# Merge gates and branch projections of a two-layer mixer, from feature-major to token-major

## The chip, the cores and the metric

One Trainium2 chip, one of its cores. The metric is the device time of one launch in microseconds (us). Three runs of the kernel before took 942.8, 944.91 and 942.83 us, median 942.83 us.

## The reference, cut to what matters

The program is a decoder trunk of two layers over 256 tokens of 1024 features in float32. Each layer has a token mixer with three branches (A: gated linear recurrence, B: gated delta rule, C: gated linear attention), each of which gives 256x512 values, and then a SwiGLU feed-forward part; a layer norm follows each of the two. The change sits where the mixer's branches are merged:

```
gates  = sigmoid(p_merge + gate_b)               # p_merge = x @ w_in[..., 3 x 1024 columns]
merged = sum(gates[:, :, gi] * (y @ w_branch[gi]) for gi, y in enumerate((ya, yb, yc)))
mix    = merged @ w_out                          # 256 x 1024
x      = layer_norm(alpha * x + mix)
```

So per layer there are three gate projections (1024 to 1024), three branch projections (512 to 1024), a product and a sum, and the output projection (1024 to 1024), called wo below.

## The kernel before, in words

**Precision.** A matmul operand a is kept as two rounded parts, a = hi + lo, and each product is three matmuls: hi by hi, lo by hi, hi by lo. Weights stream from memory in units of 128x1024 (512 KB): a DMA on SP's queue brings `raw` (4 buffers), ScalarE (ACT) copies it rounded to `hi`, and VectorE (DVE) subtracts to get `lo` (for some units in the middle of a layer GpSimd, POOL, does the subtraction instead). `unit()` hands the parts to the matmuls, and `fill()` splits units ahead of use: 6 ahead (`AHEAD`), and 14 (`FAR`) from the first branch unit of the third branch on. What is split ahead needs two of the 37 slots of 4 KB per partition, and `raw` of a later unit is fetched when an earlier one is split.

**Two orders of a matmul.** In `fm_acc` a 128x128 block of weights is the stationary operand and 256 tokens of the activations move past it: the result has features on the partitions (feature-major). In `tm_acc` a 128x128 block of activations (128 tokens) is stationary and 512 weight columns move past it: the result has tokens on the partitions (token-major), and there is one bank of PSUM for each half of the tokens (tk 0 and 1).

**The merge.** Before, gates and branches go by `fm_acc`. A gate unit pair ends in `g_chain`: ACT adds the bias, one value per partition, and takes the sigmoid in one instruction of 128x256, straight from PSUM into `gt`. A branch unit (two feature tiles, 24 matmuls) ends in `m_chain` for j = 0 to 3: DVE multiplies the PSUM tile with the gate, and from the second branch on adds it to the sum `macc`; after the third branch it splits `macc` into `mh` hi (ACT) and lo (DVE), since the sum already has features on the partitions, which is what wo needs for its stationary operand. Branches go in the order A, C, B. The list `MIX` gives the order of units.

**wo.** Its eight units go by `tm_acc`, column half n outer, the 256-row block q inner. Block q needs `mrg{q}`, the split of the quarter q of the sum, so that wo starts on the first quarter while the last is still on its way. A layer norm chain `ln_chain` for each tk follows the two halves n.

**What sets the order.** A planner (`Order.drive`) interleaves the main chain of matmuls with the spawned chains by estimated costs, and a scheduler sets the final order in which each engine issues. An engine works through its instructions in that order: one that waits holds up all behind it.

Of the kernel before, what the change touches and what calls it, by code (L numbers as in the profile page):

```python
# [20 lines left out]
P = 128  # L21
# [10 lines left out]
C_PAX, C_PAG, C_QKV, C_Z, C_SB, C_SA = 0, 512, 1024, 2560, 3072, 3076  # L32
C_CQ, C_CK, C_CV, C_CG, C_CR, C_MG = 3080, 3336, 3592, 4104, 4120, 4632

V_AW, V_AB, V_BR, V_BI, V_LAM, V_BW, V_BN, V_CG, V_CN, V_GB, V_AL, V_SM = (
    0, 16, 20, 24, 28, 32, 80, 81, 83, 84, 108, 112)
NV = 113

K_ID, K_U, K_RS, K_LM, K_BD, K_B16, K_D8, K_M32 = 0, 128, 256, 512, 768, 896, 912, 920
NK = 952  # L40


MIX = ("c0 c1 ax0 k0 k1 q0 z0 q1 ax1 v0 v1 ag0 ag1 gA0 gA1 gA2 gA3 bA0 bA1 bA2 bA3 "
       "gC0 bC0 gC1 bC1 gC2 bC2 gC3 bC3 gB0 gB1 bB0 bB1 gB2 bB2 gB3 bB3").split()
BRANCHES = "ACB"
MODE = 2

# [1 line left out]
def stream_order():  # L49
    fm = lambda c, j: [("fm", c + P * (2 * j + t)) for t in range(2)]  # L50
    tm = lambda c: [("tm", c, q) for q in range(4)]
    o = tm(C_CV) + tm(C_CR)
    base = {"q": C_QKV, "k": C_QKV + 512, "v": C_QKV + 1024, "ax": C_PAX, "ag": C_PAG,
            "c": C_CQ}
    for u in MIX:
        nm, i = u[:-1], int(u[-1])
        if nm == "z":
            o += tm(C_Z)
        elif nm in base:
            o += fm(base[nm], i)  # L60
        else:
            b = "ABC".index(nm[1])
            o += fm(C_MG + 1024 * b, i) if nm[0] == "g" else [("br", b, i)]
    o += [("wo", n, q) for n in range(2) for q in range(4)]
    o += [("f1t", q) for q in range(4)] + [("f3t", q) for q in range(4)]
    for f in range(4, NF):
        o += [("f1", f), ("f3", f)]
    o += [("f2", j) for j in range(NF)]
    return o
# [6 lines left out]
def pack(inp):  # L76
    a = {k: np.asarray(v) for k, v in inp.items()}
    f = np.float32
    w = np.empty((L, NU, P, 1024), f)
    for l in range(L):  # L80
        w_in = a["w_in"][l]
        for i, u in enumerate(ORDER):
            q = u[-1]
            if u[0] == "fm":
                src, sh = w_in[:, u[1]:u[1] + P], (8, P, P)
            elif u[0] == "tm":
                src, sh = w_in[256 * q:256 * q + 256, u[1]:u[1] + 512], (2, P, 512)
            elif u[0] == "br":
                src, sh = a["w_branch"][l, u[1]][:, 256 * q:256 * q + 256], (4, P, 256)
            elif u[0] == "wo":  # L90
                src = a["w_out"][l][256 * q:256 * q + 256, 512 * u[1]:512 * u[1] + 512]
                sh = (2, P, 512)
            elif u[0] in ("f1t", "f3t"):
                src = a["ffn_w" + u[0][1]][l][256 * q:256 * q + 256, 0:512]
                sh = (2, P, 512)
            elif u[0] == "f1":
                src, sh = a["ffn_w1"][l][:, P * q:P * q + P], (8, P, P)
            elif u[0] == "f3":
                src, sh = a["ffn_w3"][l][:, P * q:P * q + P], (8, P, P)
            else:  # L100
                src, sh = a["ffn_w2"][l][P * q:P * q + P], (1, P, D)
            w[l, i].reshape(P, sh[0], sh[2])[...] = src.reshape(sh).transpose(1, 0, 2)
    cols = list(range(C_CG, C_CG + 16)) + list(range(C_SB, C_SB + 8))
    wsm = np.ascontiguousarray(
        a["w_in"][:, :, cols].reshape(L, 8, P, 24).transpose(0, 2, 1, 3))
    vec = np.zeros((L, P, NV), f)

    def fm(x):
        return x.reshape(-1, P).T

    for l in range(L):
        v = vec[l]
        for t in range(4):
            v[:, V_AW + 4 * t:V_AW + 4 * t + 4] = fm(a["a_conv_w"][l, t])
            v[:, V_BW + 12 * t:V_BW + 12 * t + 12] = fm(a["b_conv_w"][l, t])
        v[:, V_AB:V_AB + 4] = fm(a["a_conv_b"][l])
        v[:, V_BR:V_BR + 4] = fm(a["a_b_r"][l])
        v[:, V_BI:V_BI + 4] = fm(a["a_b_i"][l])
        v[:, V_LAM:V_LAM + 4] = fm(a["a_lambda"][l])
        v[:, V_BN:V_BN + 1] = fm(a["b_norm_w"][l])  # L120
        v[:, V_CG:V_CG + 2] = fm(a["c_b_g2"][l])
        v[:, V_CN:V_CN + 1] = fm(a["c_norm_w"][l])
        v[:, V_GB:V_GB + 24] = fm(a["gate_b"][l])
        v[:, V_AL:V_AL + 4] = a["b_a_log"][l][None, :]
        v[20:24, V_SM] = a["b_dt_bias"][l]
    i = np.arange(P)
    kc = np.zeros((P, NK), f)
    kc[:, K_ID:K_ID + P] = i[:, None] == i[None, :]
    kc[:, K_U:K_U + P] = i[:, None] <= i[None, :]
    kc[:, K_RS:K_RS + 256] = (np.arange(256) % 64 != 0)[None, :]  # L130
    blk = lambda s: (i[:, None] // (2 * s) == i[None, :] // (2 * s)) & (
        i[:, None] // s != i[None, :] // s)
    for n, s in enumerate((8, 16)):
        kc[:, K_LM + P * n:K_LM + P * n + P] = blk(s) & (i[:, None] < i[None, :])
    j = np.arange(32)
    kc[:, K_BD:K_BD + P] = i[:, None] // 8 == i[None, :] // 8
    kc[:, K_B16:K_B16 + 16] = i[:, None] // 8 == np.arange(16)[None, :]
    kc[:, K_D8:K_D8 + 8] = i[:, None] % 8 == np.arange(8)[None, :]
    kc[:, K_M32:K_M32 + 32] = (i[:, None] % 32 // 8 == j[None, :] // 8) & (
        i[:, None] > j[None, :] + i[:, None] // 32 * 32)  # L140
    x = a["x"][0]
    return {
        "xtm": np.ascontiguousarray(x.reshape(2, P, D).transpose(1, 0, 2)),
        "xfm": np.ascontiguousarray(x.T.reshape(8, P, S).transpose(1, 0, 2)),
        "w": w, "wsm": wsm, "vec": vec,
        "aw": np.ascontiguousarray(np.stack([a["a_w_r"], a["a_w_i"]], 1)),
        "wg2": np.ascontiguousarray(a["c_w_g2"]),
        "lnv": np.ascontiguousarray(np.stack(
            [a["ln1_g"], a["ln1_b"], a["ln2_g"], a["ln2_b"]], 1)),
        "kc": kc,  # L150
    }
# [98 lines left out]
def _build(ctx, nc, tc, ins, out):  # L250
# [249 lines left out]
    def layer(l, xs, xtok):  # L500
# [504 lines left out]
            done("ya")  # L1005


        def g_chain(ps, b, j):
            ps = p2(ps)
            if j % 2 == 0:  # L1010
                B["gt", b, 0], B["gt", b, 1] = pair2("gt")
            gt = B["gt", b, j % 2]
            for t in range(2):
                act_fn(gt[:, t], ps[:, t], AF.Sigmoid, bias=vc(V_GB + 8 * b + 2 * j + t))
            B["gg", b, j] = gt
            done(f"gt{b}{j}")
            return
            yield

        def m_chain(ps, n, b, j, mh, ml):  # L1020
            yield k_(f"gt{b}{j}")
            ps = p2(ps)
            gt = B["gg", b, j]
            if n == 0:
                if j % 2 == 0:
                    B["macc", j], B["macc", j + 1] = pair2("macc")
                tt(B["macc", j], ps, gt, MULT)
            else:
                tt(gt, ps, gt, MULT)
                tt(B["macc", j], B["macc", j], gt, ADD)  # L1030
            if n == 2:
                split(mh[j], ml[j], B["macc", j])
                done(f"mrg{j}")

        def ln_chain(tk, halves, lv, xs_out, is_out, name):
            g, b = lv
# [159 lines left out]
        def main():  # L1196
# [17 lines left out]
            for u in MIX:  # L1214
# [7 lines left out]
                elif nm == "ag":  # L1222
                    yield from fm_pair(lambda ps: a_gate(ps, i), 1)
                elif nm == "z":
                    yield from tm_group(xs, [lambda ps, tk: silu_tm(ps, "sz", tk)], None)
                elif nm[0] == "g":
                    b = "ABC".index(nm[1])
                    yield from fm_pair(lambda ps: g_chain(ps, b, i), 1)
                else:
                    n, b = BRANCHES.index(nm[1]), "ABC".index(nm[1])  # L1230
                    if n == 2:
                        ahead[0] = FAR
                    y = ("ya", "yb", "yc")[b]
                    yield k_(y)
                    y = B[y]
                    w = unit(4)
                    ps = bank("br")
                    for t in range(2):
                        fm_acc(p2(ps)[:, t], w, y, slice(P * t, P * t + P))
                    O.spawn(m_chain(ps, n, b, i, mh, ml), 1)  # L1240
                    yield
                seen.append(u)
                if u in ("c1", "k1") and "c1" in seen and "k1" in seen:
                    O.spawn(b_inv(), 2)
# [12 lines left out]
            pw = [[bank("wo") for _ in range(2)] for _ in range(2)]  # L1257
            for tk in range(2):
                O.spawn(ln_chain(tk, pw[tk], lv, x1, False, "x1"), 0)
            seq = [(n, q) for n in range(2) for q in range(4)]  # L1260

            def wo(i, w, tk):
                n, q = seq[i]
# [3 lines left out]

            tail = 6
            for i in range(8 - tail):
                yield k_(f"mrg{i}")  # L1270
                w = unit(2)
                for tk in range(2):
                    wo(i, w, tk)
            u = []
            for tk in range(2):
                for i in range(8 - tail, 8):
                    if tk == 0:
                        if i < 4:
                            yield k_(f"mrg{i}")
                        u.append(unit(2, 1))  # L1280
                    else:
                        held[0] -= 1
# [182 lines left out]
```

## Time and profile before

| what | us |
|---|---|
| median of three runs | 942.83 |
| profiled execution, whole | 939.84 |
| its span in the trace | 938.0 |
| TensorE (PE) busy | 922.5 (98% of the span) |
| DVE busy | 644.5 (69%) |
| ACT busy | 523.6 (56%) |
| POOL busy | 162.4 (17%) |

The times worked with below come from the profiled execution. A matmul's own duration in the rows includes its way through the array and overlaps the next one, so the pace of a stream is read from the chain of waits, which lists stretches of matmuls with their count and length. The merge runs from about 160 to 262 us in the first layer and from about 618 to 722 us in the second.

### The profile page before, as it was taken

The page shows a single profiled execution, that of the slowest core. Times are in us where ns is not written, and L with a number is a line of the kernel's source. Part 1 is how long each engine was busy: PE and PEld are TensorE (multiplying, and loading weights), DVE is VectorE, ACT ScalarE, POOL GpSimd, SP SyncE. Part 2 cuts the span into 40 slices and gives each one's busy share as a digit, 9 for nine tenths or more (in the row PEclk, how much of TensorE's full clock was granted, in tenths as well). Part 3 has the DMA queues.
Part 4 walks back from the last instruction along what each step waited for, and adds up shares of the span by engine and source line. Part 5 has one row for each costly group of instructions (what it writes and reads, how often), then busy time and mean ns, then how long its engine had stood idle before and what let it go on. Part 6 is the DMA issues. An engine that isn't in the chain of part 4 may idle for free.

```text
span 938.0 us, 15814 instructions
## 1 busy us (share of the span) xinstructions
PE 922.5 (98%) x6306; PEld 838.3 (89%) x6306; DVE 644.5 (69%) x965; ACT 523.6 (56%) x824; POOL 162.4 (17%) x81
## 2 busy tenths in 40 slices
PE   7999999999999999999999999999999999999996
PEld 5998899999988888888889998999999888888885
DVE  5577975695875776676457699586768648667715
ACT  5877669644733665555145774973547147566600
POOL 0454512530000000000033351253300000000001
PEclk9999999999999999999999999999999999999998
DMA  8854324546770865568325352255568338655801
GB/s 273 266 182 148 101 69 130 173 149 234 249 290 3 299 215 180 182 240 275 111 72 191 121 158 96 72 155 195 181 217 280 132 117 271 219 180 180 286 7 45
DMA packets 47994, 162.84 MB, mean 174 GB/s; under 512 B 7537, under 2 KB 8497, under 8 KB 47793
## 3 DMA queue, kind: packets, MB, share of 16 engines
q1 hardware_dynamic: 47776, 161.71, 51.6%
q8 instruction: 49, 0.80, 0.3%
q14 instruction: 25, 0.20, 0.1%
q10 hardware_dynamic: 144, 0.13, 0.0%
HBM read 160.77 MB, written 1.05 MB: 173 GB/s over the span
## 4 chain that ended last, share of the span: by engine, by line
PE 92%; DVE 5%; DMA 1%; issue 1%; ACT 1%; POOL 0%; SPq 0%; POOLq 0%
PE fm L347 26%; PE f L347 22%; PE w L347 13%; PE tm L347 11%; PE br L347 7%; PE wo L347 5%; PE pt L347 1%; PE pp L347 1%; DVE sub L304 1%; DMA raw<-in_w_dram 1%; DVE lo L304 1%; PE pr L347 1%; PE px L355 1%; PE pln L355 1%; DVE xa L315 1%
## 5 line engine op out<-in xcount | busy, mean ns | idle before, releaser
L304 DVE TENSOR_TENSOR lo<-raw,hi 128x1024 fp32r<-128x1024 f32 (+1 forms) x241 | 310.0, 1305 | 108.9 <-ACT hi L292 101.7
L292 ACT ACTIVATE hi<-raw 128x1024 fp32r<-128x1024 f32 (+1 forms) x293 | 300.8, 1053 | 86.0 <-DMA raw<-in_w_dram 75.8
L347 PE MATMUL fm<-x,hi 128*128 128x256 f32 x1536 | 283.4, 286 | 0.0
L347 PEld LDWEIGHTS fm<-x,hi 128*128 128x128 f32 x1536 | 239.8, 192 | 2.1 <-issue 1.8
L347 PE MATMUL fm<-x,lo 128*128 128x256 f32 x768 | 217.7, 283 | 0.0
L347 PE MATMUL f<-x,hi 128*128 128x512 f32 x576 | 202.0, 396 | 0.0
L432 POOL TENSOR_TENSOR lo<-raw,hi 128x1024 fp32r<-128x1024 f32 x52 | 134.4, 2587 | 230.9 <-ACT hi L292 225.6
L347 PE MATMUL f<-x,lo 128*128 128x256 f32 x576 | 160.7, 279 | 0.0
L347 PEld LDWEIGHTS fm<-x,lo 128*128 128x128 f32 x768 | 147.4, 192 | 0.0
L347 PEld LDWEIGHTS f<-x,hi 128*128 128x128 f32 x576 | 108.1, 188 | 26.1
L347 PE MATMUL w<-hi,hh 128*128 128x512 f32 (+1 forms) x396 | 111.2, 367 | 0.0
L347 PEld LDWEIGHTS f<-x,lo 128*128 128x128 f32 x576 | 108.5, 188 | 0.1
L347 PE MATMUL tm<-hi,x 128*128 128x512 f32 x320 | 101.3, 400 | 3.6 <-ACT hi L292 3.6
L339 POOL TENSOR_TENSOR rs<-rs,mhalf 128x1 f32<-128x1 f32 x8 | 7.5, 936 | 524.2 <-DVE rs L309 524.2
L347 PEld LDWEIGHTS w<-hi,hh 128*128 128x128 f32 x396 | 71.4, 189 | 12.2
L347 PEld LDWEIGHTS tm<-hi,x 128*128 128x128 f32 x320 | 59.5, 191 | 17.0 <-ACT hi L292 5.2
L347 PE MATMUL w<-lo,hh 128*128 128x512 f32 (+1 forms) x198 | 72.4, 366 | 0.0
L347 PE MATMUL tm<-lo,x 128*128 128x512 f32 x160 | 62.3, 392 | 0.0
L347 PEld LDWEIGHTS w<-lo,hh 128*128 128x128 f32 x198 | 37.3, 188 | 6.2
L292 ACT ACTIVATE x<-pln 128x256 fp32r<-128x256 f32 x24 | 7.9, 383 | 60.7 <-PE pln L355 60.7
L347 PE MATMUL wo<-hi,mh 128*128 128x512 f32 x128 | 39.8, 392 | 0.0
L292 ACT ACTIVATE gt<-fm,vecs 128x256 f32<-128x256 f32 x48 | 20.3, 468 | 33.7 <-PE fm L347 33.6
(277 smaller groups left out, 1151.7 us busy)
## 6 DMA issues: line engine op xcount, KB each, us to landing
raw<-in_w_dram SPq DMA_DIRECT2D x291, 512.0 KB, 4.4
lnv<-in_lnv_dram SPq DMA_DIRECT2D x8, 512.0 KB, 7.4
xr<-in_xtm_dram SPq DMA_DIRECT2D x1, 1024.0 KB, 7.5
xin<-in_xfm_dram SPq DMA_DIRECT2D x3, 256.0 KB, 7.6
raw<-in_w_dram SPq DMA_DIRECT2D x2, 256.0 KB, 3.5
ar<-in_aw_dram SPq DMA_DIRECT2D x8, 64.0 KB, 4.2
out_dram<-xr SPq DMA_DIRECT2D x2, 256.0 KB, 2.1
kc<-in_kc_dram SPq DMA_DIRECT2D x1, 476.0 KB, 9.3
```

The costliest lines, as they stand in the source:

```text
L292: ins_ = A.activation(o, i, f, **k)
L304: V.tensor_tensor(out=o, in0=a, in1=b, op=op)
L315: V.scalar_tensor_tensor(out=o, in0=a, scalar=s, in1=b, op0=op0, op1=op1)
L339: G.tensor_tensor(out=o, in0=i, in1=e, op=ALU.pow)
L347: T.matmul(o, w, x, start=start, stop=stop)
L355: T.transpose(o, i, idn)
L432: G.tensor_tensor(out=lo, in0=t, in1=hi.bitcast(F32), op=SUB)
```

## The change

Gates and branch projections become token-major. The gate's bias now lies along the free dimension, so it is loaded per branch as a tile `gbias` that repeats the row on all partitions (one more DMA of 128x1024 values per branch and layer, on SP's queue), DVE adds it to the PSUM tile, and ACT takes the sigmoid from SBUF to SBUF, 128x512 at a time. A branch has two column halves j of two units each, and each half fills two banks of PSUM, one per tk. The product with the gate and the sum are done per tk on 128x512. After the third branch, each 128x512 piece of the sum (j, tk) is turned by four transposes on TensorE into a bank `pmt`, and from there split by two pairs of instructions of 128x256 into `mh`. wo goes with q outer and n inner, and waits for `mrg{j}{tk}`.

```
-MIX = ("... gA0 gA1 gA2 gA3 bA0 bA1 bA2 bA3 gC0 bC0 gC1 bC1 gC2 bC2 gC3 bC3 gB0 gB1 bB0 bB1 gB2 bB2 gB3 bB3")
+MIX = ("... gA0 gA1 bA0 bA1 gC0 bC0 gC1 bC1 gB0 gB1 bB0 bB1")
...
-        def g_chain(ps, b, j):
-            ps = p2(ps)
-            if j % 2 == 0:
-                B["gt", b, 0], B["gt", b, 1] = pair2("gt")
-            gt = B["gt", b, j % 2]
-            for t in range(2):
-                act_fn(gt[:, t], ps[:, t], AF.Sigmoid, bias=vc(V_GB + 8 * b + 2 * j + t))
...
+        def g_tm(ps, b, j, tk, bias):
+            if tk == 0:
+                B["gt", b, j] = pair("gt")
+            gt = B["gt", b, j][tk]
+            tt(gt, ps, bias[:, 512 * j:512 * j + 512], ADD)
+            yield
+            act_fn(gt, gt, AF.Sigmoid)
+            done(f"gt{b}{j}{tk}")
...
-            if n == 2:
-                split(mh[j], ml[j], B["macc", j])
-                done(f"mrg{j}")
+            tt(gt, ps, gt, MULT)
+            acc = B["macc", tk][j]
+            tt(acc, acc, gt, ADD)
+            if n == 1:
+                return
+            yield
+            pt = h4(bank("pmt"))
+            for q in range(4):
+                tp(pt[:, q], acc[:, q * P:(q + 1) * P], ident)
+            for q in range(2):
+                split(*(x[2 * j + q][:, :, tk * P:(tk + 1) * P] for x in (mh, ml)),
+                      pt[:, 2 * q:2 * q + 2])
+            done(f"mrg{j}{tk}")
...
-                    yield from fm_pair(lambda ps: g_chain(ps, b, i), 1)
+                    if i == 0:
+                        bias = slot("gbias")
+                        nc.sync.dma_start(out=bias, in_=ins["gb"][
+                            l:l + 1, 1024 * b:1024 * b + 1024].to_broadcast([P, 1024]))
+                    yield from tm_group(xs, [
+                        lambda ps, tk: g_tm(ps, b, i, tk, bias)], None)
...
-                    w = unit(4)
-                    ps = bank("br")
-                    for t in range(2):
-                        fm_acc(p2(ps)[:, t], w, y, slice(P * t, P * t + P))
-                    O.spawn(m_chain(ps, n, b, i, mh, ml), 1)
-                    yield
+                    ps = [bank("br") for _ in range(2)]
+                    for q in range(2):
+                        w = unit(2)
+                        for tk in range(2):
+                            tm_acc(ps[tk], y, tk, w, 2 * q, q == 0, q == 1)
+                        if q:
+                            for tk in range(2):
+                                O.spawn(m_tm(ps[tk], n, b, i, tk, mh, ml), 1)
+                        yield
...
-            seq = [(n, q) for n in range(2) for q in range(4)]
+            seq = [(n, q) for q in range(4) for n in range(2)]
...
-                yield k_(f"mrg{i}")
+                yield k_("mrg00"), k_("mrg01")
...
+                    if seq[i][1] == 2:
+                        yield k_(f"mrg1{tk}")
```

Counted over the whole program: 864 gate and branch matmuls of 256 columns per layer become 432 of 512 columns, with the same units of weights; each layer gets 16 transposes of 128x128, 12 bias additions of 128x512 on DVE and 3 DMAs more; 24 sigmoids of 128x256 become 12 of 128x512; 4 pairs of splits of 128x512 become 8 of 128x256.

PE at the end of the merge in the first layer, before. `br_3121` is the last branch tile, `mh_375` to `mh_378` are the four quarters of the split sum, `wo_...` the banks of wo, `hi_` and `lo_` the weights.

```order
L347 MATMUL br_3121<-ybh_2386,hi_2851 128x256 x2
L347 MATMUL br_3121<-ybh_2386,lo_2852 128x256
L347 MATMUL wo_3161<-hi_2857,mh_375 128x512 x2
L347 MATMUL wo_3161<-lo_2858,mh_375 128x512
L347 MATMUL wo_3161<-hi_2857,mh_375 128x512 x2
```

The same place on PE in the changed kernel. `br_2674` and `br_2675` are the two banks (tk 0 and 1) of the last branch column half, `macc_2131` and `macc_2133` the sums of tk 0 and tk 1, `kc_73` holds the identity.

```order
L349 MATMUL br_2675<-hi_2549,ybh_2223 128x512 x2
L349 MATMUL br_2675<-lo_2550,ybh_2223 128x512
L357 MATMUL pmt_2737<-kc_73,macc_2131 128x128 x4
L357 MATMUL pmt_2746<-kc_73,macc_2133 128x128 x4
L357 MATMUL pmt_2755<-kc_73,macc_2131 128x128 x4
L357 MATMUL pmt_2764<-kc_73,macc_2133 128x128 x4
L349 MATMUL wo_2726<-hi_2567,mh_375 128x512
L349 MATMUL wo_2728<-hi_2567,mh_375 128x512
```

Between the last branch matmul and the first of wo there are now 16 transposes, which read `macc`, and wo's first matmul reads an `mh` that comes from them; before, it read one that had been split while other branch units ran.

DVE from the product of the last branch unit on, before. `gt_3051` is the last gate tile, `lo_` are weight splits for units ahead.

```order
L304 TENSOR_TENSOR mh_377<-macc_2300,mh_377 128x512
L304 TENSOR_TENSOR gt_3051<-br_3121,gt_3051 128x512
L304 TENSOR_TENSOR macc_2300<-macc_2300,gt_3051 128x512
L304 TENSOR_TENSOR lo_3168<-raw_3024,hi_3167 128x1024
L304 TENSOR_TENSOR lo_3186<-raw_3059,hi_3185 128x1024
L304 TENSOR_TENSOR lo_3204<-raw_3089,hi_3203 128x1024
L304 TENSOR_TENSOR mh_378<-macc_2300,mh_378 128x512
```

DVE at the same place in the changed kernel, from the second instruction after the first product of branch B (`gt_2526<-br_2585`, column half 0, tk 0) on.

```order
L306 TENSOR_TENSOR gt_2653<-tm_2506,gbias_2426 128x512
L306 TENSOR_TENSOR gt_2653<-tm_2507,gbias_2426 128x512
L306 TENSOR_TENSOR lo_2657<-raw_2621,hi_2656 128x1024
L306 TENSOR_TENSOR macc_2131<-macc_2131,gt_2526 128x512
L306 TENSOR_TENSOR lo_2677<-raw_2627,hi_2676 128x1024
L306 TENSOR_TENSOR gt_2526<-br_2586,gt_2526 128x512
L306 TENSOR_TENSOR lo_2699<-raw_2633,hi_2698 128x1024
L306 TENSOR_TENSOR macc_2133<-macc_2133,gt_2526 128x512
L306 TENSOR_TENSOR gt_2653<-br_2674,gt_2653 128x512
L306 TENSOR_TENSOR gt_2653<-br_2675,gt_2653 128x512
L306 TENSOR_TENSOR macc_2131<-macc_2131,gt_2653 128x512
L306 TENSOR_TENSOR macc_2133<-macc_2133,gt_2653 128x512
```

Ahead of these rows stand the product `gt_2526<-br_2585` and two more `lo`; behind them come the halves of `mh` from `pmt`. So between the first product of branch B's column half 0 and the last sum there are now five weight splits and the two bias additions of the next gate tile, and the second layer has the same order.

## Rows read from the trace of the kernel before

**Rows 1.** The page, busy time, share of the span and instructions of each engine.

```profile
PE 922.5 (98%) x6306; PEld 838.3 (89%) x6306; DVE 644.5 (69%) x965; ACT 523.6 (56%) x824; POOL 162.4 (17%) x81
```

**Rows 2.** The page, shares of the span in the chain that ended last.

```profile
PE 92%; DVE 5%; DMA 1%; issue 1%; ACT 1%; POOL 0%; SPq 0%; POOLq 0%
```

**Rows 3.** Windows of the merges: length, busy us, granted clock, DMA share, GB/s.

```profile
147.80:262.10 114.30, 114.30 (x1009) 113.86 (x1010) 83.33 (x97) 68.91 (x95) 27.41 (x13) 1.00 0.59 195
585.80:722.40 136.60, 136.60 (x1220) 135.58 (x1220) 95.56 (x112) 87.08 (x126) 33.65 (x13) 1.00 0.55 181
```

**Rows 4.** The chain of waits: start us, length us, engine, tile, line, count.

```profile
71.29 10.91 PE tm L347 x48
...
116.13 1.24 DVE Y L304
...
124.67 0.87 PE pyf L355 x8
...
180.59 11.51 PE br L347 x96
...
227.53 11.52 PE fm L347 x96
239.04 5.76 PE br L347 x48
...
262.08 19.97 PE wo L347 x88
282.06 0.58 PE pln L355 x4
```

**Rows 5.** DVE's timeline, end of the first merge: start us, length us, instruction, count.

```profile
245.50 2.35 DVE L304 TENSOR_TENSOR lo<-raw,hi 128x1024 fp32r<-128x1024 f32 x2
247.77 0.68 DVE L304 TENSOR_TENSOR gt<-br,gt 128x512 f32<-128x512 f32 x1
248.37 1.21 DVE L304 TENSOR_TENSOR lo<-raw,hi 128x1024 fp32r<-128x1024 f32 x1
...
264.34 0.68 DVE L304 TENSOR_TENSOR mh<-macc,mh 128x512 fp32r<-128x512 f32 x1
264.94 0.68 DVE L304 TENSOR_TENSOR gt<-br,gt 128x512 f32<-128x512 f32 x1
265.66 0.69 DVE L304 TENSOR_TENSOR macc<-macc,gt 128x512 f32<-128x512 f32 x1
...
270.67 0.68 DVE L304 TENSOR_TENSOR mh<-macc,mh 128x512 fp32r<-128x512 f32 x1
```

**Rows 6.** ACT and DVE timelines, a split of 128x256 from transposed PSUM.

```profile
300.02 0.38 ACT L292 ACTIVATE hh<-pht 128x256 fp32r<-128x256 f32 x1 [2.55 <-PE pht L355]
300.44 0.42 DVE L304 TENSOR_TENSOR hh<-pht,hh 128x256 fp32r<-128x256 f32 x1 [2.18 <-ACT hh L292]
```

**Rows 7.** PE's timeline, an idle stretch of 2.27 us in the first layer.

```profile
117.51 1.94 PE L355 MATMUL px<-kc,Y 128*128 128x128 f32 x8 [2.27 <-DVE Y L304]
```

**Rows 8.** Windows around it, columns as in rows 3.

```profile
116.00:117.00 1.00, 0.00 (x0) 0.00 (x0) 0.97 (x2) 0.00 (x0) 0.00 (x0) 1.00 0.00 0
117.00:118.00 1.00, 0.49 (x3) 0.52 (x4) 1.00 (x4) 0.00 (x0) 0.00 (x0) 0.61 0.00 0
118.00:119.00 1.00, 1.00 (x6) 1.00 (x5) 1.00 (x5) 0.37 (x1) 0.00 (x0) 0.50 0.00 0
119.00:120.00 1.00, 1.00 (x7) 1.00 (x6) 1.00 (x3) 0.74 (x3) 0.00 (x0) 0.50 0.00 0
120.00:121.00 1.00, 1.00 (x8) 1.00 (x8) 1.00 (x2) 1.00 (x3) 0.00 (x0) 0.69 0.00 0
```

**Rows 9.** The gate sigmoids: nanoseconds least, median, most; first and last start.

```profile
L292 ACT ACTIVATE gt<-fm,vecs x48: 452/468/482, 160.6 to 724.1; 128x256 f32<-128x256 f32 x48
```

**Rows 10.** The page, DMA issues: count, KB each, median us to landing.

```profile
raw<-in_w_dram SPq DMA_DIRECT2D x291, 512.0 KB, 4.4
lnv<-in_lnv_dram SPq DMA_DIRECT2D x8, 512.0 KB, 7.4
```

More of the change, by code (lines that the diff above doesn't have):

```diff
@@ L33 @@
 C_CQ, C_CK, C_CV, C_CG, C_CR, C_MG = 3080, 3336, 3592, 4104, 4120, 4632
-V_AW, V_AB, V_BR, V_BI, V_LAM, V_BW, V_BN, V_CG, V_CN, V_GB, V_AL, V_SM = (
-    0, 16, 20, 24, 28, 32, 80, 81, 83, 84, 108, 112)
-NV = 113
+V_AW, V_AB, V_BR, V_BI, V_LAM, V_BW, V_BN, V_CG, V_CN, V_AL, V_SM = (
+    0, 16, 20, 24, 28, 32, 80, 81, 83, 84, 88)
+NV = 89
 K_ID, K_U, K_RS, K_LM, K_BD, K_B16, K_D8, K_M32 = 0, 128, 256, 512, 768, 896, 912, 920
 NK = 952
-MIX = ("c0 c1 ax0 k0 k1 q0 z0 q1 ax1 v0 v1 ag0 ag1 gA0 gA1 gA2 gA3 bA0 bA1 bA2 bA3 "
-       "gC0 bC0 gC1 bC1 gC2 bC2 gC3 bC3 gB0 gB1 bB0 bB1 gB2 bB2 gB3 bB3").split()
+MIX = ("c0 c1 ax0 k0 k1 q0 z0 q1 ax1 v0 v1 ag0 ag1 gA0 gA1 bA0 bA1 gC0 bC0 gC1 bC1 "
+       "gB0 gB1 bB0 bB1").split()
 BRANCHES = "ACB"
@@ L62, in stream_order @@
             b = "ABC".index(nm[1])
-            o += fm(C_MG + 1024 * b, i) if nm[0] == "g" else [("br", b, i)]
-    o += [("wo", n, q) for n in range(2) for q in range(4)]
+            o += tm(C_MG + 1024 * b + 512 * i) if nm[0] == "g" else [
+                ("br", b, i, q) for q in range(2)]
+    o += [("wo", n, q) for q in range(4) for n in range(2)]
     o += [("f1t", q) for q in range(4)] + [("f3t", q) for q in range(4)]
@@ L88, in pack @@
             elif u[0] == "br":
-                src, sh = a["w_branch"][l, u[1]][:, 256 * q:256 * q + 256], (4, P, 256)
+                src = a["w_branch"][l, u[1]][256 * q:256 * q + 256, 512 * u[2]:512 * u[2] + 512]
+                sh = (2, P, 512)
             elif u[0] == "wo":
@@ L122, in pack @@
         v[:, V_CN:V_CN + 1] = fm(a["c_norm_w"][l])
-        v[:, V_GB:V_GB + 24] = fm(a["gate_b"][l])
         v[:, V_AL:V_AL + 4] = a["b_a_log"][l][None, :]
@@ L147, in pack @@
         "wg2": np.ascontiguousarray(a["c_w_g2"]),
+        "gb": np.ascontiguousarray(a["gate_b"]),
         "lnv": np.ascontiguousarray(np.stack(
@@ L1005, in a_chain, with m_tm @@
             done("ya")
-        def g_chain(ps, b, j):
-            ps = p2(ps)
-            if j % 2 == 0:
-                B["gt", b, 0], B["gt", b, 1] = pair2("gt")
-            gt = B["gt", b, j % 2]
-            for t in range(2):
-                act_fn(gt[:, t], ps[:, t], AF.Sigmoid, bias=vc(V_GB + 8 * b + 2 * j + t))
-            B["gg", b, j] = gt
-            done(f"gt{b}{j}")
-            return
-            yield
[L1020 to L1023, printed above, removed]
-            if n == 0:
[L1025 to L1030, printed above, removed]
-            if n == 2:
-                split(mh[j], ml[j], B["macc", j])
-                done(f"mrg{j}")
+        def g_tm(ps, b, j, tk, bias):
[3 more added lines that the diff above has]
+            tt(gt, ps, bias[:, 512 * j:512 * j + 512], ADD)
+            yield
+            act_fn(gt, gt, AF.Sigmoid)
+            done(f"gt{b}{j}{tk}")
+        def m_tm(ps, n, b, j, tk, mh, ml):
+            yield k_(f"gt{b}{j}{tk}")
+            gt = B["gt", b, j][tk]
+            if n == 0:
+                if j == 0:
+                    B["macc", tk] = pair("macc")
+                tt(B["macc", tk][j], ps, gt, MULT)
+                return
[3 more added lines that the diff above has]
+            if n == 1:
+                return
+            yield
[6 more added lines that the diff above has]
+            done(f"mrg{j}{tk}")
         def ln_chain(tk, halves, lv, xs_out, is_out, name):
@@ L1276, in main @@
                 for i in range(8 - tail, 8):
+                    if seq[i][1] == 2:
+                        yield k_(f"mrg1{tk}")
                     if tk == 0:
-                        if i < 4:
-                            yield k_(f"mrg{i}")
                         u.append(unit(2, 1))
```

## The prediction

> **What bounds the kernel now.** I read the busy times first. TensorE (PE) is busy 98% of the span, DVE 69%, ACT 56% [rows 1], and the chain that ended last is 92% PE [rows 2]. An average over the launch does not tell about the merge, so the windows of the two merges come next: in 147.80 to 262.10 and 585.80 to 722.40 PE is busy for the whole of the stretch at a granted clock of 1.00, while DVE has 83 of 114 us and ACT 69 of 114 [rows 3]. There PE's work is the time, and other engines count only where they make it wait. The chain of waits then gives PE's pace and shows that wo starts at 262.08, right where the last branch matmuls end [rows 4]. Last, DVE's timeline shows what still had to be done for wo at that moment [rows 5].
>
> **The pace, the gain.** In the chain, 96 matmuls of 256 columns take 11.51 and 11.52 us, 119.9 ns each, whether branch or gate; 48 of 512 columns take 10.91 us, 227.3 ns each, and 88 of wo take 19.97 us, 226.9 ns each [rows 4]. The 512-column rows already have activations as the stationary operand, as the changed matmuls have. Two of 256 cost 239.8 ns, one of 512 some 227.1: 12.7 ns less. There are 432 such pairs per layer: 5.5 us a layer, 11.0 us in all, with 10.8 and 11.1 by the two 512-column rows. All of it is on the path, since PE has no idle time there.
>
> A rule of the Trainium skill speaks against this. "TensorE: Matmul & The Clock Gate", section "Back-to-back issue gap", gives an isolated matmul N/2.4 + 2.5 ns for N columns, with a fixed part of 2.5 ns; by that formula (an estimate from the page) the pairs would save only 2.2 us. The rows have a fixed part of about 13 ns (119.9 less 256/2.4 is 13.2, 227.1 less 512/2.4 is 13.8), and the page itself says that its formula is not the pace of a stream, so the rows decide.
>
> **What is added beside PE.** Twelve bias additions of 128x512 per layer cost DVE about 0.6 us each (start to start, 247.77 to 248.37 [rows 5]), 7.3 us; the window has 31 us of DVE idle [rows 3]. ACT has 24 gate sigmoids of 0.468 us per layer now [rows 9], 11.2 us; twelve of double width take between that and its half. Three DMAs of 512 KB per layer go on SP's queue, ahead of weights: the nearest, `lnv`, lands in 7.4 us and `raw` in 4.4 [rows 10], with the DMA engines 0.59 and 0.55 busy [rows 3]; the bias is needed only after 48 matmuls (10.9 us). I take 0 for all three, hidden by PE's work; were the cover gone, one late bias would cost at most 7.4 us, and a faster start of weights could not help an engine that is never idle, so the lower end is 0. wo keeps its 96 matmuls; its new order moves the transposes of the layer norm by some ten matmuls, at 0, within one such group, 0.58 us [rows 4].
>
> **What moves onto the path.** Before, wo could begin at 262.08 because three quarters of `mh` were split while other branch units ran. Only the last quarter was late: its product started at 264.94, its sum at 265.66, its last split at 270.67, ready at 271.35 [rows 5]. wo needed it only after 50 matmuls, 11.4 us, that is at 273.4: nothing was lost.
>
> In the changed kernel every wo matmul needs rows of `mh` that come out of transposes, and all 16 transposes stand on PE ahead of wo. The last two groups of four read the two sums of branch B's column half 1. Call T the end of the last branch matmul. DVE's queue, from the product of column half 0, tk 0, to the last sum, holds 15 instructions: five `lo` and ten of 128x512. That first product waits for a matmul with 30 behind it until T, so it can start at T less 6.8 us, plus the hand-over (0.14 us between DVE's `Y` ending at 117.37 and PE's 117.51 [rows 4, 7]): T - 6.6. A `lo` queued behind another takes 1.14 us (245.50 to 247.77 for two), a 128x512 operation 0.60 queued and 0.72 if it waits for the one before it (264.34, 264.94, 265.66) [rows 5]. Five by 1.15 and ten by 0.61 are 11.85 us: the last sum is ready at T + 5.2. Four transposes take 0.44 (eight in 0.87 [rows 4]), so PE is done with them near T + 5.7, while DVE and ACT have split the earlier pieces; a split is 0.38 on ACT and 0.42 on DVE [rows 6], and the first quarter comes from the first groups.
>
> So PE loses 5.7 us per layer, of which 16 transposes are 1.75 and some 4 us idle, the longest piece from the first group (about T + 0.4) to the second (its sum at T + 2.8). Why the `lo` stand there: the wide lead of 14 units starts at branch B's first unit. Before, that was at 239.04, 23 us ahead of wo [rows 4]; now only 48 matmuls, 10.9 us, remain, and the splits for wo's weights crowd into them.
>
> The bounds of this term: if DVE had nothing queued at T, there would still be a product (0.60), a sum (0.72), transposes (0.44), a split (0.80) and hand-overs (0.6): 3.2 us. If the last `raw` comes late, its 4.4 us to landing start at a slot freed late in branch B, and the stall goes to about 8. I take 5.7, the sum of the queue as it is written.
>
> **The clock.** The one comparable idle of PE before, 2.27 us ahead of 117.51 [rows 7], was followed by a granted clock of 0.61, 0.50, 0.50 and 0.69 in the four windows from 117 on, having been 1.00 in 116 to 117 [rows 8]: 2.4 GHz, then 1.2 GHz. Work lost: 0.39 + 0.50 + 0.50 + 0.31 = 1.7 us. The new stall has an idle piece of that length and a second of over 1 us. I take 1.4 per layer, since transposes and waits fill part of the slow time; the ends are 0 and 1.7.
>
> **The sum.** Per layer: -5.5 + 5.7 + 1.4 = +1.6; both: +3.2. On the profiled execution's 939.84 that is 943.0; the median of the runs, 942.83, lies 3.0 above that execution, so against the median: 946.0.
>
> **The rivals.**
> - *Stall without the clock's fall.* The transposes come in between, so that no idle piece is as long as that of 2.27 us. Then +0.4: 943.2. For: the longest piece is close to it. Against: rows 7 and 8 are the only example, and it fell.
> - *DVE keeps up* (the other side, faster). The planner's rows are an order, not times: if ACT and DMA run ahead, so that splits and bias additions in the queue are done before branch B's products are ready, the stall is the 3.2 us of the bare chain, without the clock's fall: 2 x (-5.5 + 3.2) = -4.6, 938.2. It decides from the point where fewer than two of the five `lo` remain behind the first product. Against: the product of column half 0 is itself ahead of all five in the queue.
> - *Weights late.* The last `raw` lands after T and the `lo` behind it holds the sums, as the queue is in order: stall 8 instead of 5.7, both layers: 946.0 + 4.6 = 950.6. For: slots come free only as PE goes on, and `raw` has a median of 4.4 us. Against: DMA is 0.59 busy.
> - *The wider matmuls bring little.* If the pace of 512 columns is kept up only elsewhere and a pair saves nothing here, the gain of 11 is gone: 957. Against: three streams at 227 ns. By the skill's 2.5 ns above it would be 954.8, an estimate from that page.
>
> **How the numbers follow.** A difference of 0.3%, 2.8 us, is about what can be told from no change: 940.0 to 945.7. Forecast: 0.42, from 944.5 to 948, of which 0.10 lies under 945.7. Stall without the clock: 0.29, no difference. DVE keeps up: 0.14, faster. Weights late: 0.13, slower. No gain of the pace: 0.02, slower. Faster 0.14, same 0.10 + 0.29 = 0.39, slower 0.32 + 0.13 + 0.02 = 0.47. The range from 938 to 952 takes in the rivals to both sides but the last; the forecast's own is 944.5 to 948.
>
> **What would show it.** In the changed profile: gate and branch stretches at 227 ns per matmul, nothing idle on PE before the last branch unit; then 16 `pmt` transposes with idle time ahead of groups 2 and 3 put down to DVE, wo starting 5 to 6.5 us after the last branch matmul in both layers; a clock near 0.5 for some us behind it. A wo that starts within 3.5 us of T, or idle PE at the gates' start (a late bias), would show the reasoning wrong.

## The result, and the profile after

The changed kernel took 948.66 us (median of 8 runs, 946.06 to 951.28), the kernel before 942.62 us on the same chips (8 runs, 940.59 to 944.91): a ratio of 1.0068, 95% interval 1.0054 to 1.0082, so it is 6.0 us slower. A second set gave 948.47 against 941.34, ratio 1.0076 (1.0055 to 1.0096). The prediction was 946.0, slower, range 938 to 952. The profiled execution of the changed kernel took 950.33 us (span 948.5), 1.7 above its median, and that of the kernel before 939.84, 2.8 below its own; so the traces lie 10.5 us apart where the medians lie 6.0 apart, and sums from the two traces have to be read with that.

First the pace, which answers to [rows 4]. The chain of waits of the changed kernel, columns as there:

```profile
179.78 10.89 PE br L349 x48
...
207.89 10.88 PE tm L349 x48
...
250.58 6.03 DMA raw<-in_w_dram
256.71 1.07 ACT hi L294
...
261.37 1.20 DVE gt L306 x2
263.22 1.97 PE pmt L357 x8
265.19 19.54 PE wo L349 x78
```

48 branch or gate matmuls of 512 columns take 10.89 and 10.88 us, 226.8 ns each: the gain is there in full, and the windows of the two merges, which end 0.7 and 2.0 us before the last branch matmul does, show PE busy all but 0.4 us, as in [rows 3]:

```profile
147.00:256.00 109.00, 109.00 (x582) 91.19 (x581) 78.99 (x101) 66.35 (x80) 34.59 (x13) 1.00 0.62 213
585.00:718.00 133.00, 132.62 (x808) 114.28 (x808) 95.67 (x120) 82.50 (x111) 32.94 (x13) 1.00 0.55 188
```

What follows in the chain is new: at the end of the merge it leaves PE and goes through a transfer of weights, a rounding copy, DVE, and back to PE. PE's timeline shows the stall itself; the bracket gives the idle time ahead and what ended it. The last branch matmul in each layer, then the groups of transposes and wo:

```profile
256.46 0.39 PE L349 MATMUL br<-lo,ybh 128*128 128x512 f32 x1
257.72 0.66 PE L357 MATMUL pmt<-kc,macc 128*128 128x128 f32 x4 [0.87 <-DVE macc L306]
261.42 0.66 PE L357 MATMUL pmt<-kc,macc 128*128 128x128 f32 x4 [3.04 <-DVE macc L306]
263.22 1.97 PE L357 MATMUL pmt<-kc,macc 128*128 128x128 f32 x8 [1.14 <-DVE macc L306]
264.84 2.06 PE L349 MATMUL wo<-hi,mh 128*128 128x512 f32 x4
...
719.79 0.39 PE L349 MATMUL br<-lo,ybh 128*128 128x512 f32 x1
721.29 0.66 PE L357 MATMUL pmt<-kc,macc 128*128 128x128 f32 x4 [1.11 <-DVE macc L306]
725.40 1.12 PE L357 MATMUL pmt<-kc,macc 128*128 128x128 f32 x4 [3.45 <-DVE macc L306]
727.19 1.97 PE L357 MATMUL pmt<-kc,macc 128*128 128x128 f32 x8 [0.68 <-DVE macc L306]
728.81 1.63 PE L349 MATMUL wo<-hi,mh 128*128 128x512 f32 x3
```

With 0.23 us for the last branch matmul, T is 256.69 and 720.02; wo starts 8.15 and 8.79 us later, of which 5.05 and 5.24 us are idle. The same stretch on DVE, which answers to [rows 5], in the first layer:

```profile
250.47 0.69 DVE L306 TENSOR_TENSOR gt<-br,gt 128x512 f32<-128x512 f32 x1
251.93 1.23 DVE L306 TENSOR_TENSOR lo<-raw,hi 128x1024 fp32r<-128x1024 f32 x1 [0.78 <-ACT hi L294]
253.51 1.23 DVE L306 TENSOR_TENSOR lo<-raw,hi 128x1024 fp32r<-128x1024 f32 x1 [0.35 <-ACT hi L294]
254.65 1.28 DVE L306 TENSOR_TENSOR gt<-tm,gbias 128x512 f32<-128x512 f32 x2
255.85 1.22 DVE L306 TENSOR_TENSOR lo<-raw,hi 128x1024 fp32r<-128x1024 f32 x1
256.98 0.69 DVE L306 TENSOR_TENSOR macc<-macc,gt 128x512 f32<-128x512 f32 x1
257.80 1.23 DVE L306 TENSOR_TENSOR lo<-raw,hi 128x1024 fp32r<-128x1024 f32 x1
258.94 0.69 DVE L306 TENSOR_TENSOR gt<-br,gt 128x512 f32<-128x512 f32 x1
259.55 1.22 DVE L306 TENSOR_TENSOR lo<-raw,hi 128x1024 fp32r<-128x1024 f32 x1
260.68 0.69 DVE L306 TENSOR_TENSOR macc<-macc,gt 128x512 f32<-128x512 f32 x1
261.28 1.28 DVE L306 TENSOR_TENSOR gt<-br,gt 128x512 f32<-128x512 f32 x2
262.48 1.29 DVE L306 TENSOR_TENSOR macc<-macc,gt 128x512 f32<-128x512 f32 x2
```

These are the 15 instructions that the prediction counted, with their durations. What it did not have are the waits between them: each `lo` needs the rounded copy of a weight unit, and the copy needs the transfer. The last sum ends at 263.77, T + 7.1, not T + 5.2: the queue starts 0.4 us after the T - 6.6 that was worked out, the waits in brackets are 1.1 us, and the rest are small gaps.

The clock in windows of one microsecond, columns as in [rows 3]:

```profile
262.00:263.00 1.00, 0.08 (x1) 0.00 (x0) 1.00 (x2) 0.38 (x1) 0.00 (x0) 0.57 0.81 279
...
268.00:269.00 1.00, 1.00 (x4) 0.81 (x3) 0.42 (x2) 0.05 (x1) 0.00 (x0) 0.51 0.99 369
269.00:270.00 1.00, 1.00 (x6) 0.83 (x5) 0.16 (x1) 0.00 (x0) 0.00 (x0) 1.00 0.93 311
```

In both layers the granted clock falls to 0.5 (1.2 GHz), as at the idle piece of [rows 7, 8]: in the first right after the idle piece of 3.04 us, for some 6.8 us, in the second already within the piece of 3.45 us, for some 10. The eight last transposes take 1.97 us where eight took 0.87, and wo's first matmuls run at half rate: from its first matmul to the first of the feed-forward part wo takes 24.7 us (264.84 to 289.55) where it took 22.8 (261.92 to 284.68).

What was costed at nothing was hidden: `gbias` lands in a median of 4.5 us and no wait of PE names it, the bias additions take 0.68 us each, and the sigmoids 0.63 us (median, 24 of them), 7.6 us per layer where it was 11.2.

### The profile page after: what moved, and what is told of

It is laid out like the page before. It is cut to its first block, busy times and chain, and to the rows that moved or that the text cites. A ratio compares the mean times of both kernels' runs of the same rounds, so it can differ in the third digit from the quotient of the medians.

```text
span 948.5 us, 14155 instructions
## 1 busy us (share of the span) xinstructions
PE 923.3 (97%) x5474; PEld 802.0 (85%) x5474; DVE 650.2 (69%) x997; ACT 521.3 (55%) x808; POOL 170.0 (18%) x81
## 4 chain that ended last, share of the span: by engine, by line
PE 83%; DVE 8%; DMA 4%; ACT 3%; issue 1%; POOL 0%; SPq 0%; POOLq 0%; ACTq 0%
PE tm L349 22%; PE f L349 21%; PE w L349 13%; PE fm L349 10%; PE wo L349 5%; PE br L349 5%; DMA raw<-in_w_dram 4%; DVE lo L306 2%; ACT hi L294 1%; DVE sub L306 1%; PE pt L349 1%; PE pp L349 1%; PE pln L357 1%; DVE xa L317 1%; DVE gt L306 1%
## 5 line engine op out<-in xcount | busy, mean ns | idle before, releaser
L306 DVE TENSOR_TENSOR lo<-raw,hi 128x1024 fp32r<-128x1024 f32 (+1 forms) x241 | 305.3, 1283 | 93.3 <-ACT hi L294 82.9
L349 PE MATMUL tm<-hi,x 128*128 128x512 f32 x704 | 221.8, 397 | 2.6 <-ACT hi L294 2.6
L434 POOL TENSOR_TENSOR lo<-raw,hi 128x1024 fp32r<-128x1024 f32 x52 | 141.0, 2715 | 219.9 <-ACT hi L294 204.0
L349 PEld LDWEIGHTS tm<-hi,x 128*128 128x128 f32 x704 | 130.9, 190 | 30.5 <-ACT hi L294 4.3
L349 PE MATMUL fm<-x,hi 128*128 128x256 f32 x768 | 143.5, 288 | 0.0
L349 PE MATMUL tm<-lo,x 128*128 128x512 f32 x352 | 137.6, 392 | 0.1
L349 PEld LDWEIGHTS fm<-x,hi 128*128 128x128 f32 x768 | 120.8, 193 | 1.8 <-issue 1.8
L349 PE MATMUL fm<-x,lo 128*128 128x256 f32 x384 | 109.5, 285 | 0.0
L349 PEld LDWEIGHTS tm<-lo,x 128*128 128x128 f32 x352 | 66.6, 189 | 14.9 <-DVE lo L306 0.7
L349 PEld LDWEIGHTS fm<-x,lo 128*128 128x128 f32 x384 | 74.2, 193 | 0.0
```

The source lines that it names most:

```text
L306: V.tensor_tensor(out=o, in0=a, in1=b, op=op)
L349: T.matmul(o, w, x, start=start, stop=stop)
L434: G.tensor_tensor(out=lo, in0=t, in1=hi.bitcast(F32), op=SUB)
```

## The experiments

Theory "queue": wo waits for DVE, which works through weight splits queued between the products and the sums of branch B. Rivals: "chain" (the product, sum, transposes and split take that long by themselves), "weights" (the transfers set it), and, for a part, the clock. Each kernel starts from the changed one, if not said otherwise, and ratios are to runs of the kernel before on the same chip.

### The lead later

```
-                    if n == 2:
-                        ahead[0] = FAR
...
                     if seq[i][1] == 2:
                         yield k_(f"mrg1{tk}")
+                        ahead[0] = FAR
```

> The wide lead of 14 units begins only when the last quarter sums are split (in wo), not at branch B's first unit. So none of the weight splits stands between the products and the sums of branch B on DVE. Theory 'queue' (the splits of weights queued between the sums make the stall): wo starts about 2 us after the last branch matmul in place of 8.2 and 8.8, the granted clock stays at 1.00, and the time is 936 to 938 us. Rival 'chain' (product, sum, transposes and split take that long by themselves): wo still starts 3.2 us or more after it, with a half clock, 942 to 944. Rival 'weights' (the lead is needed there): wo or the feed-forward part waits for weights, 946 or more.

955.63 us, ratio 1.0148 (1.0127 to 1.017): worse than the change. The place in dispute did what "queue" says: the first transposes follow the last branch matmul at 256.44 without a wait and wo starts at 257.51, T + 1.1. But the splits were now inside wo, ahead of DVE's work for the layer norm. PE's timeline behind wo:

```profile
284.28 0.99 PE L357 MATMUL pln<-kc,xr 128*128 128x128 f32 x4 [3.61 <-issue]
286.24 1.08 PE L357 MATMUL pln<-kc,xr 128*128 128x128 f32 x4 [0.98 <-DVE xr L317]
289.28 1.09 PE L357 MATMUL pln<-kc,xr 128*128 128x128 f32 x4 [1.96 <-DVE xr L317]
```

So 6.5 us of idle time came back at the norm, and the granted clock fell to 0.5 again, from 284 to 294. The first wait is put down to no engine here; in the second layer the same wait, 3.38 us, names DVE's `xr`. DVE's statistics for the norm stand at 277.28 and 279.07, with weight splits before, between and behind them. "Queue" holds for the stall, and my time for this kernel was wrong since I asked only who waits at the old place for the splits, not who waits at the new one.

### Column half 0 first

```
-       "gB0 gB1 bB0 bB1").split()
+       "gB0 bB0 gB1 bB1").split()
```

> Only the order of branch B's units is changed: gate and branch of column half 0, then of column half 1, so that half 0 is summed 11 us earlier; the weight splits stay where the lead of 14 puts them. wo's first 36 matmuls need half 0 alone. Theory 'queue': half 1's product, sum and splits fall under these 36 matmuls (8.2 us); the first wo matmul waits only for splits of half 0, which stand behind half 1's products on DVE, some 2 to 2.5 us; 936 to 939 us. Rival 'chain': the wait for half 1 comes back inside wo, a stall of 3 us or more there, 942 to 945.

941.68 us, ratio 0.9999 (0.9982 to 1.0016). Slower than I expected by 3 us, faster than the change by 7. PE's only waits at the end of the first merge:

```profile
259.49 1.01 PE L349 MATMUL wo<-hi,mh 128*128 128x512 f32 x3 [1.78 <-ACT mh L294]
261.57 0.79 PE L349 MATMUL wo<-hi,mh 128*128 128x512 f32 x1 [1.08 <-DVE mh L306]
```

ACT's timeline ahead of the first of them:

```profile
258.04 1.13 ACT L294 ACTIVATE gt<-gt 128x512 f32<-128x512 f32 x2
259.08 0.64 ACT L294 ACTIVATE mh<-pmt 128x256 fp32r<-128x256 f32 x2
```

So the two waits have two causes: the first copies of half 0's split stand on ACT behind the two sigmoids of the last gate tile (1.78 us), and the subtractions that go with them stand on DVE behind half 1's products and one of its sums (1.08 us). Together they are 2.9 us, a little over the 2 to 2.5 expected of DVE alone; half 1 itself came in time. What the expectation left out is the clock, which falls to 0.5 here too, from 261 to 267.7 (mean 0.81 from 255 to 273, as in the changed kernel). "Chain" would have put a wait of 3 us or more inside wo.

### Both

The edits of the two above.

> Both of these edits. Half 0's transposes then stand among the gate matmuls of half 1, and wo starts without a wait. If the gain of the wider matmuls is 11.0 us and the 32 transposes cost 3.5, and nothing else is lost, the time is 942.6 - 11.0 + 3.5 = 935.1. If the pace brings little, as the rival with 2.5 ns had it, it is about 944.

956.62 us, ratio 1.0161 (1.0147 to 1.0175). No wait at wo's start, and the waits of the first experiment at the norm (3.48, 0.92 and 2.02 us). That is 21 us above the 935.1 expected, and it says nothing on the gain, as the later lead hides it.

### The clock kept up

```
-            pt = h4(bank("pmt"))
+            pt = bank("pmt")
+            for _ in range((0, 12, 4, 0)[2 * j + tk]):
+                T.matmul(pt, keep[0][:, 0:P], keep[0], start=True, stop=True)
+            pt = h4(pt)
```

> The changed kernel with 12 dummy matmuls of 128x512 in bf16 ahead of the second group of transposes and 4 ahead of the third, which fill the idle time of the stall (3.0 to 3.5 us and 0.7 to 1.1 us) and whose result is overwritten; the stall's own length is not touched. If the clock's fall costs what the trace of the changed kernel lets one add up (8 transposes in 1.97 us in place of 0.87, and some 4 us of wo at half rate, 2.9 to 3.3 us per layer), the time falls by about 6 us to 942.7. If my estimate of 1.4 us per layer was the right size, to 945.9. If the clock falls all the same, no change.

944.97 us, ratio 1.0046 (1.0029 to 1.0063). PE's timeline:

```profile
261.48 0.66 PE L357 MATMUL pmt<-kc,macc 128*128 128x128 f32 x4 [0.22 <-DVE macc L306]
263.28 1.26 PE L357 MATMUL pmt<-kc,macc 128*128 128x128 f32 x8 [0.28 <-DVE macc L306]
```

The sums still come late, the eight last transposes take 1.26 us in place of 1.97, and the window from 255 to 273 has a mean granted clock of 1.00 where the changed kernel has 0.81. Against the changed kernel run again (below), the distance to the kernel before falls from 7.1 to 3.4 us: the half clock costs 3.7 us, 1.9 per layer, between the two sizes expected and nearer to the 1.4 of the prediction. The intervals of the two ratios, 1.6 and 1.9 us to each side, leave that figure rough, and the stall was not quite the same: wo starts 6.6 and 7.8 us after T here and 7.8 and 8.5 in the changed kernel run again, of which the transposes at full clock explain 0.7 each, so in the first layer the sums also came sooner. The trace of the changed kernel adds up to more: 0.7 us in the transposes (1.97 against 1.26) and 2.0 in wo (24.7 against 22.8), about 2.7 per layer.

### The changed kernel again

> The changed kernel itself, once more, beside the next three on one chip, so that they and the kernel with the clock kept up (944.97) can be set against it. By the first result 6 us above the kernel before, about 948. If it is 945 here, the clock kept up brought nothing.

948.47 us, ratio 1.0076 (1.0055 to 1.0096), and wo's waits as in the first profile (3.07 and 1.14 us ahead of the second and third groups).

### Half of the splits to POOL

```
-PMOD, PLO, PHI = 2, 8, 60
+PMOD, PLO, PHI = 2, 8, 88
```

> The changed kernel with every second weight split of units 60 to 87 on POOL in place of DVE, as units 8 to 59 have it; order of units and lead as they were. Between branch B's first product and the last sum two weight splits stand on DVE in place of five. Theory 'queue': the last sum comes near T + 3 (products of the last matmuls at T + 0.2, then two products and two sums), wo starts 3.5 to 4 us after T in place of 8.2 and 8.8, and the time is 937 to 940. Rival 'weights late' (the splits, on whichever engine, wait for raw from memory, and the sums for them): wo starts 6 us or more after T, 943 or more.

952.49 us, ratio 1.0122 (1.0095 to 1.0149), with wo at 269.19, 9.1 us after T: neither theory's reason, though the time is on the side of the rival. DVE's timeline:

```profile
256.35 0.68 DVE L306 TENSOR_TENSOR gt<-br,gt 128x512 f32<-128x512 f32 x1
257.70 2.09 DVE L306 TENSOR_TENSOR lo<-raw,hi 128x1024 fp32r<-128x1024 f32 x1 [0.66 <-ACT hi L294]
259.71 1.27 DVE L306 TENSOR_TENSOR gt<-tm,gbias 128x512 f32<-128x512 f32 x2
260.91 1.66 DVE L306 TENSOR_TENSOR macc<-macc,gt 128x512 f32<-128x512 f32 x1
...
264.23 2.82 DVE L306 TENSOR_TENSOR macc<-macc,gt 128x512 f32<-128x512 f32 x1
```

and POOL's at the same time:

```profile
256.17 2.53 POOL L434 TENSOR_TENSOR lo<-raw,hi 128x1024 fp32r<-128x1024 f32 x1 [2.15 <-ACT hi L294]
259.43 2.60 POOL L434 TENSOR_TENSOR lo<-raw,hi 128x1024 fp32r<-128x1024 f32 x1 [0.72 <-ACT hi L294]
263.74 2.76 POOL L434 TENSOR_TENSOR lo<-raw,hi 128x1024 fp32r<-128x1024 f32 x1 [1.72 <-PE pmt L357]
```

While POOL subtracts, DVE's operations on two tensors in SBUF stand still: the sum at 264.23, 0.69 us by itself, ends at 267.05, 0.55 us after POOL's subtraction that ran from 263.74 to 266.50, and the `lo` at 257.70 ends 1.1 us after the one that ended at 258.70. The three operations held up (257.70, 260.91, 264.23) lose 4.0 us together. The queue is shorter in instructions and longer in time.

### Half 0 first, the lead in two steps

```
-       "gB0 gB1 bB0 bB1").split()
+       "gB0 bB0 gB1 bB1").split()
...
-                        ahead[0] = FAR
+                        ahead[0] = FAR if i else 9
...
-                                O.spawn(m_tm(ps[tk], n, b, i, tk, mh, ml), 1)
+                                O.spawn(m_tm(ps[tk], n, b, i, tk, mh, ml), 0 if n == 2 else 1)
```

> Half 0 first; the lead goes to 9 units at branch B's first unit and to 14 at its column half 1; the merge of branch B has the planner's first priority. Half 0 is then summed and transposed beside the gate matmuls of half 1, wo starts without a wait, and the weight splits come before the norm. All splits stay on DVE, and ten of them stand ahead of the bias additions of the last gate tile. If they are done by T + 3, no wait: 942.6 - 11.0 + 3.5 = 935. If they hold up half 1 beyond its cover of 36 matmuls, a wait of 2 to 4 us inside wo per layer: 939 to 943.

935.71 us, ratio 0.9941 (0.9921 to 0.9961): faster than both kernels, and at the 935 of "no wait". The chain of waits at the end of the second merge is PE alone:

```profile
701.61 0.87 PE pmt L357 x8
702.48 8.18 PE tm L349 x36
710.66 5.44 PE br L349 x24
716.10 8.16 PE wo L349 x36
724.26 0.87 PE pmt L357 x8
```

Half 0 is transposed while gate matmuls run, half 1 after 36 matmuls of wo, in 0.87 us per group of eight at full clock. In the first layer nine splits stand between half 0's sums and the last gate's bias additions and hold these until 261.56, T + 2.6, but within the cover.

### The same with POOL

The two edits of MIX and the lead, at the old priority, with POOL's share of the splits.

> As e7, but with every second weight split of units 60 to 87 on POOL, and the merge at its old priority. Theory 'queue': no wait at wo's start nor inside it; the gain of the pace less the transposes is left, 935. Rival 'weights late': a wait inside wo all the same, 939 or more.

940.32 us, ratio 0.9987 (0.9969 to 1.0004), with waits of 0.93 and 0.49 us in the first layer and 1.41 and 0.49 in the second: 4.6 us slower than the ramped kernel, from which it differs in the priority too, so POOL's part of that is not separated.

### Five buffers for raw weights

```
-RAW, AHEAD, FAR, SLACK, SLOTS = 4, 6, 14, 1.5, 37
+RAW, AHEAD, FAR, SLACK, SLOTS = 5, 6, 14, 1.5, 37
```

> The changed kernel with five buffers for raw weights in place of four; DVE's queue at the end of branch B stays as it is (five weight splits and ten operations of 128x512). In the changed kernel's trace DVE stood idle 1.1 us (layer 1) and 0.45 us (layer 2) inside that queue, waiting for rounded copies whose raw came late, and started it 0.4 and 1.9 us after the time I had worked out. If the loop of raw transfers (landing, copy, split, next issue) sets this, a fifth buffer takes most of it away: wo starts 6 to 7 us after the last branch matmul in place of 8.2 and 8.8, and the time is 944 to 946. If the queue's own work is all, it stays at 948.

941.08 us, ratio 0.9994 (0.9976 to 1.0011), 7 us under the changed kernel. The queue did not stay quite as the text has it: the scheduler put one split ahead of the first product, so four remain behind it. In the first layer, where T is 258.4:

```profile
251.83 0.69 DVE L306 TENSOR_TENSOR gt<-br,gt 128x512 f32<-128x512 f32 x1 [0.46 <-PE br L349]
...
261.18 1.28 DVE L306 TENSOR_TENSOR macc<-macc,gt 128x512 f32<-128x512 f32 x2
```

No wait for a copy is left in the queue. It starts at T - 6.6, as worked out, and four splits and ten operations end 10.6 us later, at T + 4.0: the working of the prediction with one split less. wo starts at 262.93, T + 4.5, and the clock stays at 1.00. In the second layer the queue starts late (its first product waits behind splits whose raw took 6.77 us), wo starts 6.1 us after T, and the clock falls (mean 0.83 from 715 to 735). So both are shown: the queue's work is the larger part of the stall, and the loop of transfers, copies and splits adds to it. Of the 3.7 us by which the first layer's stall is shorter, the split that moved ahead is 1.15, the waits and the late start are 1.5 and the transposes at full clock 0.7; the run does not part the fifth buffer from the order that came with it.

### The lead earlier

```
+                    if u == "gB0":
+                        ahead[0] = FAR
...
-                    if n == 2:
-                        ahead[0] = FAR
```

> The changed kernel with the lead of 14 from the first gate unit of branch B on (some 33 us ahead of wo, where it was 11), the order of units untouched. Two weight splits in place of five stand between branch B's first product and the last sum, and the transposes of half 1 move into wo. Theory 'queue': the last sum at T + 2, wo at about T + 2.7, the clock stays at 1.00; 938. Rival 'weights late' (the two splits wait for their raw, since slots come free only as TensorE goes on): wo at T + 4 or later with a lower clock, 942 or more.

939.32 us, ratio 0.9961 (0.9948 to 0.9974). PE's waits, first layer:

```profile
261.82 0.96 PE L349 MATMUL wo<-hi,mh 128*128 128x512 f32 x3 [0.24 <-ACT mh L294]
264.82 0.50 PE L349 MATMUL wo<-hi,mh 128*128 128x512 f32 x1 [2.03 <-DVE mh L306]
```

wo starts at 261.11, 1.4 us after T (259.7), and then waits 0.2 and 2.0 us, with the clock at 1.00. The order of units is that of the change, the edit moves only when the weights are split, and the loss is gone. With it the scheduler moved half 1's transposes into wo, to 270.87, so part of the gain can be the cover that the last sums have there. "Queue", a little dearer than expected.

### Five buffers elsewhere

The edit of the fifth buffer, on the kernel before and on the ramped kernel.

> The kernel before with five buffers for raw weights: a control for the run of the changed kernel with five, which was 7 us faster than with four. If that came from the end of the merges alone, the kernel before gains nothing, 941 to 942.5. If the fifth buffer helps elsewhere in the launch, it gains that here too: 937 to 939 would mean that half of the 7 us has nothing to do with the change.

940.88 us, ratio 0.9985 (0.9976 to 0.9994): the fifth buffer is worth 1.3 us to the kernel before, so most of the 7 us belongs to the merge's end.

> The ramped kernel with half 0 first (935.7) with five buffers for raw weights. TensorE had no idle time left at the end of its merges, so by the theory 'queue' the fifth buffer can only bring what it brings the kernel before elsewhere: 933 to 936.

931.9 us, ratio 0.9891 (0.9878 to 0.9905): the fastest of all, 10.3 us under the kernel before and 1.1 under the range that I expected. Between the profiled executions of the two ramped kernels the difference, 3.1 us at the start of the feed-forward part, lies ahead of the merge, in the first 120 us, where that with four buffers has one more wait, 2.1 us for `pR`, of its own; whether that is the buffer or one execution is open.

## Why the prediction was right, and where it was off

- **The gain of the pace**, 5.5 us per layer: right. T moved from 261.92, where wo's first matmul started before (the chain's 262.08 has the last matmul's way through the array in it), to 256.69 in the first layer, 5.2 us, and in the second the stretch from the first matmuls of `px` to T went from 137.28 us (584.99 to 722.27) to 132.01 (588.01 to 720.02), 5.3 us. Without the stall, gain less transposes is 11.0 - 3.5 = 7.5 us; the ramped kernel has 5.6 of it, and that with five buffers 9.0 (10.3 less the 1.3 that the buffer is worth to the kernel before); the 1.5 us above 7.5 are not accounted for.
- **What was costed at nothing**: right, as shown above; wo's new order costs nothing visible.
- **The stall**, 5.7 us: the right place, the right engine and the right instructions, but 8.15 and 8.79 us, outside the 5 to 6.5 us given as its sign; about 0.7 us of it are transposes at half clock. The step that failed is the sum "five by 1.15 and ten by 0.61": it took each split to be ready when its turn came. The splits wait for copies and these for transfers, which land in 4.1 to 6.0 us here with four buffers in turn, and in the second layer DVE began the queue at T - 4.7 (its first product stands at 715.35), not T - 6.6. Late start and waits are 0.4 and 1.1 us in the first layer, 1.9 and 0.45 in the second. The rival "weights late", with its price of 8 us and a chance of 0.13, named this, and a `raw` that lands after T is seen in the second layer (722.32, T + 2.3), where DVE then waits 0.29 us; in truth it came on top of the queue and not in its place. The five buffers show it: with them the first layer follows the working with one split less to 0.1 us.
- **The clock**, 1.4 us per layer: fell as forecast, but cost more than the upper end of 1.7: 1.9 by the runs with and without dummy matmuls, about 2.7 by the trace. [Rows 7] was not the only such idle piece before: 2.68 us ahead of a matmul at 11.59 was followed by 0.70, 0.50, 0.50 and 0.59 in the windows from 11 on. The rival of a stall **without the clock's fall** falls with this.
- **The sum**: +1.6 per layer forecast, +3.0 measured (6.0 for both). The forecast gain and the forecast stall nearly cancel, so an error of 1.5 us in the stall doubles the difference; the sign was safe only with the clock's term. 948.66 lies above the forecast's own 944.5 to 948, and inside the range since that was drawn to take in "weights late". In the two traces the terms come to more: -5.2 + 8.1 + 2.0 = +4.9 in the first layer and -5.3 + 8.8 + 2.0 = +5.5 in the second, nearly all of the 10.5 us between the spans. Which of them is smaller in an execution near the median, no run shows.
- **DVE keeps up**, the rival on the faster side: false for the kernel as it is, and true of the ramped kernel, where the splits come out of the way. The rival of **no gain** from wider matmuls fell with the first row of the chain.

## What to carry to other kernels

A layout that makes TensorE's stream faster may move a dependent step (here transposes and a split) from the side of the stream to its seam; price the seam by the whole in-order queue ahead of the last result, with the transfers that its instructions wait for, and not by the step alone. Then cure it by order: finish part of the reduction early enough that the next stage can begin on that part, and place work done ahead of need where no late result stands behind it, asking at the new place too who stands behind it.

## What was not expected of the hardware

DVE and POOL slowed each other: POOL's `lo` took 2.76 us at 263.74 where one that had begun with DVE idle (248.25) took 2.40, and with POOL subtracting, DVE's `lo` took 1.92 us in the mean (7 of them between 240 and 270) where it took 1.23 in the changed kernel (13), and a sum up to 2.82 in place of 0.69. Only operations with both inputs in SBUF were hit; `gt<-br` at 256.35 and the two `gt<-tm,gbias` at 259.71, with one input in PSUM, kept their 0.68 and 0.6 us while POOL was at work. The Trainium skill ("SBUF — State Buffer", section "SBUF: two separate sides") says that a DVE operation with two SBUF inputs and a GpSimd one that reads SBUF contend for a pair of ports, which the first to start keeps for its whole instruction. The rows agree, to the 0.55 us that a sum still takes once POOL is done.
